# RWKV-7 / RG-LRU decoder step: two branch results kept in DRAM, weight halves asked for one tile ahead, sample steps spread over two units

## The chip, the cores and the metric

One NeuronCore of a Trainium2 chip runs the whole step as one program. The metric is device time in microseconds (us), lower is better. PE is TensorE's matmul stream, PEld its weight loads, DVE is VectorE, ACT is ScalarE, POOL is GpSimd, and SP is the queue of SyncE, which here issues every DMA. Instructions of one queue run in the order in which they stand in it; a waiting instruction holds all that stand behind it.

## The reference

One decoder layer in float32 for a prompt of 1024 tokens and 8 samples of one token each, which share all weights (D_MODEL 1024, D_FF 2816):

```python
def _layer(h, mk, mv, S0, shift0, h0, buf0, P):
    h = _layer_norm(DN_ALPHA * h + 0.5 * _swiglu(h, P['ffn1_wi'], P['ffn1_wo']), ...)
    mix, S_new, shift_new, h_new, buf_new = _mixer(h, S0, shift0, h0, buf0, P)
    h = _layer_norm(DN_ALPHA * h + mix, ...)
    h = _layer_norm(DN_ALPHA * h + _xattn(h, mk, mv, P['xa_wq'], P['xa_wo']), ...)
    h = _layer_norm(DN_ALPHA * h + 0.5 * _swiglu(h, P['ffn2_wi'], P['ffn2_wo']), ...)
```

The change is in the mixer, whose end is

```python
    yn = ((y - ym) * lax.rsqrt(yv + GN_EPS)).reshape(B, T, W) * gn_g + gn_b
    bonus = (jnp.sum(rh * kh * r_k, axis=-1, keepdims=True) * vh).reshape(B, T, W)
    rwkv_out = (yn + bonus) * g
    lru_out = hs * jax.nn.gelu(p_gelu)
    gates = jax.nn.sigmoid(p_gate).reshape(B, T, N_BRANCH, D_MODEL)
    merged = gates[:, :, 0] * rwkv_out + gates[:, :, 1] * lru_out
    out = merged @ P['w_mix_out']
```

Here `y` is the output of the RWKV-7 state recurrence and `hs` that of the RG-LRU branch. For a sample, one step of the recurrence is applied to its own 64 x 64 states: multiply by the decay, subtract and add outer products, read out.

## The kernel before

Activations lie transposed, channels on the 128 partitions and 1032 token columns (1024 prompt, 8 samples) along the free axis. A float32 product is made of three matmuls of two split halves (`mm3`, L125 to L127): hi x hi, hi x lo, lo x hi. A weight half of 128 x 512 is fetched by SP into a tile `raw` (L94), rounded by ACT into `wh` (L99), and DVE takes the rest, `wl` (L100); `split_half` does these three. A weight tile of 128 output channels is two such halves (`load_split`). `S.rawseq` and `S.hlseq` say which pools the next `raw` and the next `wh`, `wl` come from.

The program runs feed-forward 1, mixer, cross attention, feed-forward 2. In the mixer, channels are cut into 8 pairs of heads (p = 0 to 7), two of them at a time are a group g, and the prompt into 4 blocks n of 256 columns. A unit t = 4 g + n is one block of one group, so there are 16. One round per unit weaves these streams:

- `stage_unit` prepares unit t + 1 from the projections in the DRAM scratch `GD[p]` (tile `R`, `za`), and makes the bonus term `bv`;
- `inverse` solves the triangular systems of unit t, 31 dependent pairs of DVE instructions (`pr`, `tq`);
- `chain` runs the state recurrence of unit t - 1, and `post` normalises its output (`ysb`), adds `bv`, applies the gates `tg` and adds the branch's `lm`;
- `branches` makes the RG-LRU branch (`cb`, `ge`, `xc`, result `lm`) of unit t - 1;
- `samples_b` applies the samples' step, in rounds with n = 3, for both pairs of the group; for each pair and each half of the samples it needs five rows of DRAM scratch (`row`, L1142, tile `wt`, each as two DMAs) one after the other;
- `gemms` is the filler: the remaining input projections (`project`, tile `g`, stored by SP as `GD<-ev`, L639) and then the output projection (`out_proj`, `FD<-ev`).

`weave` and `rounds` set the order in which the code writes these; the framework's scheduler then sets each engine's queue, and every tile's pool says how many buffers it has and so which earlier reader a new writer waits for. Until the change, the filler had one `raw` buffer and three of `wh` and `wl`:

```python
        S.rawseq, S.hlseq = itertools.cycle([S.wraw]), itertools.cycle([S.whl])
```

The same two settings serve what comes after the rounds: `out_last` (last part of the output projection, with `f` and `acc` read from DRAM), its LayerNorm, and `memory_kv`, which makes keys and values of the 256 memory tokens (PSUM tile `kv`, weights `wk` and `wv`, results `mo` and `vo`), all woven into one another.

Of the kernel before, what the change touches and what calls it, by code (L numbers as in the profile page):

```python
# [10 lines left out]
F32 = mybir.dt.float32  # L11
F32R = mybir.dt.float32r
AF = mybir.ActivationFunctionType
ALU = mybir.AluOpType
# [5 lines left out]
NT = NP + NS  # L20
DFF = 2816
KT = D // 128
# [510 lines left out]
DRAM = bass.MemoryType.DRAM  # L533
GR, GK, GV, GZ, GA, GL, GE, G1, G0, GG = range(10)

FILL = [42] * 11 + [37] * 5

LATE = ("ev", "ref", "dend", "scl", "sm", "wsb", "sf", "ysb", "gsq", "ivc", "bv", "lm")


def mixer(octx, S, I, O, MG, HD, pre):
# [13 lines left out]
    with ExitStack() as ctx:  # L555
# [66 lines left out]
        FD = S.dram.tile([8, 128, NT], F32, name="FD")  # L622
        GD = [S.dram.tile([128, 10, NT], F32, name="GD%d" % p) for p in range(8)]

        def cols(w, c0, n, q, kt=KT):
            yield from settled(S, c0, n)
            for k in range(kt):
                mm3(nc, q, wblock(w, k), S.HH[:, k, c0:c0 + n], S.HL[:, k, c0:c0 + n], k == 0, k == kt - 1)
                if k % 2:
                    yield  # L630

        def project(p, mt, gi, func, sc, w, cs, psg, pool):

            for c0, n in cs:
                q = psg(n)
                yield from cols(w, c0, n, q)
                e = pool.tile([128, 344], F32, tag="ev", name="ev", bufs=2)[:, :n]
                ACT(e, q, func, scale=sc)
                nc.sync.dma_start(out=GD[p][:, gi, c0:c0 + n], in_=e)  # L639

# [15 lines left out]
        def gemms():  # L656


            for g in range(S.npairs // 2):
                ps_ = (2 * g, 2 * g + 1)  # L660
                for xs, early in (((0, 1, 2), True), ((3, 4, 5), False), ((6,), False)):
                    if g or not early:
                        for p in ps_:
                            for x in (tiles(p)[i] for i in xs):
                                yield from project(p, *x, load_split(S, I["w_in"][x[0]]), CH3, psg, t1)
                                ready.add((p, x[1]))
                            if 6 not in xs:
                                ends(p, early)
            ready.add("h")
            yield from out_proj()  # L670

# [108 lines left out]
        def stage(U, i):  # L780
# [52 lines left out]
            P.bv.append(bv)  # L833
            yield
# [122 lines left out]
        def branch(p, n, P):  # L957
# [38 lines left out]
            STT(gi, gi, 0.5, th, ALU.mult, ALU.mult)  # L996
            S.lm_live += 1
            assert S.lm_live <= 4
            hs = tmp("lm", 264, 4)
            nc.vector.tensor_tensor_scan(out=hs[:, 0:256], data0=gr[:, 0:256], data1=gi[:, 0:256],  # L1000
# [13 lines left out]
            STT(hs, ge[:, 1], 1.0, hs, ALU.add, ALU.mult)  # L1014
            P.lm.append(hs)
            if n == 3:
# [7 lines left out]
        def post(p, n, Y):  # L1024

            col = lambda t: t[:, p:p + 1]
            c0, P = NCW[n][0], Ps[p]
            while (p, G0) not in ready:
                yield
            tg = t1.tile([128, 2, 256], F32, tag="tg", name="tg")  # L1030
            nc.sync.dma_start(out=tg, in_=GD[p][:, G0:GG + 1, c0:c0 + 256])
# [10 lines left out]
            STT(ysb, ysb, col(V["gnb"]), P.bv[n][:, 0:256], ALU.add, ALU.add)  # L1042
            STT(tg[:, 0], tg[:, 0], 1.0, tg[:, 1], ALU.add, ALU.mult)
            yield
            while len(P.lm) <= n:
                yield
            STT(ysb, ysb, 0.5, tg[:, 0], ALU.mult, ALU.mult)
            STT(ysb, P.lm[n][:, 0:256], 0.5, ysb, ALU.mult, ALU.add)
            S.lm_live -= 1
# [79 lines left out]
        def samples_b(p, P):  # L1129

            y, T3 = tmp("y8", 8, 4, t1), P.T3
            P.y8 = y
            sv = P.sv
            b8 = lambda t: t.unsqueeze(2).to_broadcast([128, 4, 64])
            for b0 in (0, 4):
                B = slice(b0, b0 + 4)
                s_, t_ = (ta.tile([128, 4, 64], F32, tag=x, name=x) for x in ("ws", "wt"))
                nc.sync.dma_start(out=s_, in_=I["srwkv"][p].rearrange("p (b k) -> p b k", k=64)[:, B])

                def row(j):  # L1140
                    for h in range(2):
                        nc.sync.dma_start(out=t_[half[h]], in_=T3[8 * j + b0:8 * j + b0 + 4, 64 * h:64 * h + 64].unsqueeze(  # L1142
                            0).to_broadcast([64, 4, 64]))
                    return t_
# [7 lines left out]
                row(1)  # L1152
                yield
                TTo(s_, s_, t_, ALU.mult)
                row(4)
                yield
                TTo(t_, t_, b8(yb), ALU.mult)
                TTo(s_, s_, t_, ALU.subtract)
                row(2)
                yield  # L1160
                TTo(t_, t_, b8(sv[:, 5, B]), ALU.mult)
                TTo(s_, s_, t_, ALU.add)
                nc.sync.dma_start(out=O["srwkv"][p].rearrange("p (b k) -> p b k", k=64)[:, B], in_=s_)
                row(0)
                yield
                TTo(t_, s_, t_, ALU.mult)
                nc.vector.tensor_reduce(out=yb, in_=t_, axis=mybir.AxisListType.X, op=ALU.add)

# [30 lines left out]

        def out_proj():  # L1200

            kt = KT - 2
            for m in range(KT):
                w_ = load_split(S, I["w_mix"][m])
                for c0, n in CH3:
# [9 lines left out]
                    q = psg(n)  # L1215
                    yield from cols(w_, c0, n, q, kt)
                    e = tmp("ev", 344, 2)[:, :n]
# [28 lines left out]
        def stage_unit(t):  # L1246
            g, n = divmod(t, 4)
            U = SimpleNamespace(p0=2 * g, n=n, TT=TTs[t % 2], AR=[], SC=[], BK=[])
            if n == 0:
                U.ref = tmp("ref", 34, 2).rearrange("p (i c) -> p i c", i=2)  # L1250
                U.dend = tmp("dend", 32, 2).rearrange("p (i c) -> p i c", i=2)
                nc.vector.memset(U.ref[:, :, 16:17], 0.0)
                Ps.extend(SimpleNamespace(bv=[], lm=[]) for _ in range(2))
            else:
                U.ref, U.dend = units[-1].ref, units[-1].dend
# [26 lines left out]
        nu = 2 * S.npairs  # L1282
        nbr = S.lm_live = 0
        late_steps = []
        fill = gemms()
        rounds(13, [(stage_unit(0), 34), (part(fill, 42), 42)], late_steps, True)
        for t in range(nu):
# [405 lines left out]
```

## Time and profile before

| | |
|---|---|
| median of 3 runs | 3322.96 us (3314.7 to 3323.16) |
| profiled execution | 3323.29 us, of which the span from first to last instruction is 3321.4 us |
| mean granted TensorE clock | 0.942 of full speed |
| feed-forward 1, 0 to 660 us | PE busy 649.56 of 660 us, clock 1.00 |
| mixer's units, 860 to 2020 us | PE busy 1070.29 of 1160 us, clock 0.92 |
| last unit, 2020 to 2100 us | PE busy 53.65 of 80 us, clock 0.68 |
| end of the mixer, 2100 to 2200 us | PE busy 77.69 of 100 us, clock 0.81 |
| memory values, 2200 to 2280 us | PE busy 58.27 of 80 us, clock 0.58 |
| feed-forward 2, from 2640 us | PE busy 660.97 of 681 us, clock 0.98 |

Times in the profile count from the first instruction. "Busy" is the time in which an engine has an instruction in execution, and an instruction at half clock is busy for longer. "Idle before" is the time an engine stood still ahead of an instruction, with what ended it behind an arrow. The granted clock in a window is the mean over it.

### The profile page before, as it was taken

To read this page: it belongs to the slowest core of one execution; us is meant where nothing else is said; L and a number is where in the kernel's file an instruction comes from. 1 tells how busy PE (TensorE), PEld (TensorE's weight loads), DVE (VectorE), ACT (ScalarE), POOL (GpSimd) and SP (SyncE) were. 2 spreads that over 40 slices of the span, in tenths; PEclk is the share of its full clock that TensorE was granted. 3 is DMA by queue.
4 is the path that set the end of the run, shared out by engine and by line. 5 is a ranking of instruction groups with operands and counts; after the bars stand their busy time and mean duration, and the time that the engine had idled before them with its cause. 6 is when DMAs were issued, how large, how long until landed. Compare 5 with 4: busy or idle time off the path is not lost. (4 is left out here: it accounts for less than half of the span.)

```text
span 3321.4 us, 63119 instructions
## 1 busy us (share of the span) xinstructions
PE 3080.6 (93%) x23324; PEld 2896.4 (87%) x23324; DVE 2199.0 (66%) x5895; ACT 1433.5 (43%) x3190; POOL 554.5 (17%) x526
## 2 busy tenths in 40 slices
PE   8999999999999989989998987778898999999997
PEld 8999999989988878878887776667788899999997
DVE  7666665573377776778876777533768666666556
ACT  5333351145555555556554654343334433334112
POOL 2222201130000101100110100440003422220111
PEclk9999999999999999999998888768999999999998
DMA  4222253225433444444344444523533222225321
GB/s 136 77 78 80 84 166 112 87 80 175 152 108 105 123 128 120 112 117 139 104 123 121 115 115 136 161 84 118 153 121 120 79 77 77 80 80 163 112 83 52
DMA packets 364036, 369.93 MB, mean 111 GB/s; under 512 B 143024, under 2 KB 264912, under 8 KB 363728
## 3 DMA queue, kind: packets, MB, share of 16 engines
q1 hardware_dynamic: 363728, 365.91, 37.0%
q8 instruction: 183, 3.00, 0.4%
q14 instruction: 125, 1.02, 0.1%
HBM read 269.15 MB, written 96.84 MB: 110 GB/s over the span
## 5 line engine op out<-in xcount | busy, mean ns | idle before, releaser
L125 PE MATMUL ps<-HH,wh 128*128 128x258 f32 (+1 forms) x2384 | 718.4, 302 | 16.6 <-ACT HH L508 7.4
L126 PE MATMUL ps<-HL,wh 128*128 128x258 f32 (+1 forms) x2384 | 716.8, 301 | 0.6 <-POOL HL L215 0.6
L127 PE MATMUL ps<-HH,wl 128*128 128x258 f32 (+1 forms) x2384 | 715.6, 300 | 0.0
L125 PE MATMUL g<-HH,wh 128*128 128x344 f32 (+2 forms) x1840 | 628.9, 342 | 19.7 <-ACT wh L99 5.4
L126 PE MATMUL g<-HL,wh 128*128 128x344 f32 (+2 forms) x1840 | 602.2, 328 | 1.3 <-DVE HL L548 1.3
L127 PE MATMUL g<-HH,wl 128*128 128x344 f32 (+2 forms) x1840 | 598.8, 327 | 4.8 <-DVE wl L100 4.8
L125 PEld LDWEIGHTS ps<-HH,wh 128*128 128x128 f32 x2384 | 451.4, 189 | 18.7 <-ACT HH L508 7.4
L126 PEld LDWEIGHTS ps<-HL,wh 128*128 128x128 f32 x2384 | 451.0, 189 | 1.4 <-POOL HL L215 0.9
L127 PEld LDWEIGHTS ps<-HH,wl 128*128 128x128 f32 x2384 | 450.5, 189 | 0.0
L125 PEld LDWEIGHTS g<-HH,wh 128*128 128x128 f32 x1840 | 361.7, 197 | 39.8 <-ACT wh L99 9.7
L127 PEld LDWEIGHTS g<-HH,wl 128*128 128x128 f32 x1840 | 360.4, 196 | 12.2 <-DVE wl L100 7.9
L126 PEld LDWEIGHTS g<-HL,wh 128*128 128x128 f32 x1840 | 361.9, 197 | 7.6 <-DVE HL L548 3.5
L228 ACT ACTIVATE wh<-raw 128x512 fp32r<-128x512 f32 x280 | 176.5, 631 | 322.2 <-PE ps L126 259.5
L100 DVE TENSOR_TENSOR wl<-raw,wh 128x512 fp32r<-128x512 f32 x302 | 214.0, 714 | 152.9 <-ACT wh L99 150.7
L99 ACT ACTIVATE wh<-raw 128x512 fp32r<-128x512 f32 x302 | 185.9, 626 | 294.8 <-PE ps L126 77.2
L334 POOL TENSOR_TENSOR raw<-raw 128x512 f32<-128x512 f32 x160 | 213.8, 1336 | 566.1 <-DVE wl L229 372.6
L229 DVE TENSOR_TENSOR wl<-raw,wh 128x512 fp32r<-128x512 f32 x280 | 203.8, 729 | 139.6 <-ACT wh L228 132.7
L442 DVE SCALAR_TENSOR_TENSOR acc<-ps,acc 128x344 f32<-128x344 f32 x336 | 168.5, 512 | 144.2 <-PE ps L127 143.6
L548 DVE TENSOR_TENSOR pr<-tq,iv 128x2 f32<-128x2 f32 (+30 forms) x496 | 160.8, 324 | 3.0
L553 ACT ACTIVATE ev<-g 128x344 f32<-128x344 f32 x192 | 87.3, 455 | 133.0 <-PE g L127 108.1
L917 DVE TENSOR_REDUCE tq<-pr 128x1 f32<-128x2 f32 (+30 forms) x496 | 121.6, 245 | 2.9
L374 ACT ACTIVATE g<-g 128x258 f32<-128x258 f32 x160 | 67.1, 419 | 112.9 <-DVE g L333 112.0
(410 smaller groups left out, 6444.9 us busy)
## 6 DMA issues: line engine op xcount, KB each, us to landing
raw<-in_wi_dram SPq DMA_DIRECT2D x176, 256.0 KB, 2.8
raw<-in_w_in_dram SPq DMA_DIRECT2D x116, 256.0 KB, 3.4
GD<-ev SPq DMA_DIRECT2D x168, 172.0 KB, 1.9
raw<-in_wo_dram SPq DMA_DIRECT2D x104, 256.0 KB, 3.1
raw<-HID SPq DMA_DIRECT2D x88, 258.0 KB, 3.1
HID<-g SPq DMA_DIRECT2D x80, 258.0 KB, 2.1
wt<-T SPq DMA_DIRECT2D x160, 64.0 KB, 2.7
GD<-t SPq DMA_DIRECT2D x24, 344.0 KB, 3.5
```

The costliest lines, as they stand in the source:

```text
L99: nc.scalar.activation(out=hi, in_=raw, func=AF.Identity)
L100: nc.vector.tensor_tensor(out=lo, in0=raw, in1=hi.bitcast(F32), op=ALU.subtract)
L125: nc.tensor.matmul(ps, wh, xh, start=first, stop=False)
L126: nc.tensor.matmul(ps, wh, xl, start=False, stop=False)
L127: nc.tensor.matmul(ps, wl, xh, start=False, stop=last)
L228: nc.scalar.activation(out=hi, in_=x, func=AF.Identity)
L229: nc.vector.tensor_tensor(out=lo, in0=x, in1=hi.bitcast(F32), op=ALU.subtract)
L334: pool_tt = lambda o, a, b, op: nc.gpsimd.tensor_tensor(out=o, in0=a, in1=b, op=op)
L442: nc.vector.scalar_tensor_tensor(out=a, in0=q, scalar=0.5 / ALPHA, in1=a, op0=ALU.mult, op1=ALU.add)
L548: TTo = lambda o, a, b, op: nc.vector.tensor_tensor(out=o, in0=a, in1=b, op=op)
L553: ACT = lambda o, a, f=AF.Identity, **kw: nc.scalar.activation(out=o, in_=a, func=f, **kw)
L917: nc.vector.tensor_reduce(out=tq[:, 0:m, i], in_=pv, axis=mybir.AxisListType.X, op=ALU.add)
```

## The change

It does five things, all in the mixer.

- `bv` (32 stores of 128 x 256) and `lm` (32 stores) go to two new planes of `GD[p]`, GB and GM; `post` reads them back with the gates, in one DMA of four planes in place of two, and begins only when the branch's block is there. Their tiles shrink from 8 to 2 and from 4 to 2 buffers.
- A fourth buffer of `wh` and `wl` is put into the filler's cycle, and `project` and `out_proj` ask for one half of the next weight tile after the matmuls of the first and of the second of their three column chunks, instead of both halves ahead of the tile.
- `row` has two buffers, and rows are fetched two at a time, ahead of their use.
- `samples_b` runs for one pair in the round with n = 3 and for the other in the round after it; in the last round still for both.
- After the rounds, two more `raw` buffers and one more of `wh` and `wl` (`more_weights`).

```diff
-GR, GK, GV, GZ, GA, GL, GE, G1, G0, GG = range(10)
+GR, GK, GV, GZ, GA, GL, GE, G1, G0, GG, GB, GM = range(12)
...
-        def project(p, mt, gi, func, sc, w, cs, psg, pool):
+        def project(p, mt, gi, func, sc, w, cs, psg, pool, then=None):
             for c0, n in cs:
                 q = psg(n)
                 yield from cols(w, c0, n, q)
+                if then and c0 < CH3[2][0]:
+                    then()
                 e = pool.tile([128, 344], F32, tag="ev", name="ev", bufs=2)[:, :n]
...
+            queue = itertools.chain(((W[j], x[:, 512 * i:512 * i + 512]) for j, x in enumerate(src) for i in range(2)))
+            def load():
+                for to, x in itertools.islice(queue, 1):
+                    to.append(split_half(S, x))
+            load()
+            load()
+            for j, (p, x, i) in enumerate(todo):
+                yield from project(p, *x, W[j], CH3, psg, t1, load)
...
-        S.rawseq, S.hlseq = itertools.cycle([S.wraw]), itertools.cycle([S.whl])
+        S.rawseq = itertools.cycle([S.wraw])
+        S.hlseq = itertools.cycle([S.whl] * 3 + [actx.enter_context(tc.tile_pool(name="mwhl", bufs=1))])
...
-            bv = tmp("bv", 256, 8)
+            bv = tmp("bv", 256, 2)
             TTo(bv, xv[:, 0:256], pb[:, 0:256], ALU.mult)
+            nc.sync.dma_start(out=GD[p][:, GB, c0:c0 + 256], in_=bv)
...
-            hs = tmp("lm", 264, 4)
+            hs = tmp("lm", 264, 2)
...
-            P.lm.append(hs)
+            nc.sync.dma_start(out=GD[p][:, GM, c0:c0 + 256], in_=hs[:, 0:256])
+            P.lm.append(n)
...
-            while (p, G0) not in ready:
+            while (p, G0) not in ready or n not in P.lm:
                 yield
-            tg = t1.tile([128, 2, 256], F32, tag="tg", name="tg")
-            nc.sync.dma_start(out=tg, in_=GD[p][:, G0:GG + 1, c0:c0 + 256])
+            tg = t1.tile([128, 4, 256], F32, tag="tg", name="tg")
+            nc.sync.dma_start(out=tg, in_=GD[p][:, G0:GM + 1, c0:c0 + 256])
...
                 def row(j):
+                    t = ta.tile([128, 4, 64], F32, tag="wt", name="wt", bufs=2)
                     for h in range(2):
...
-                row(3)
-                yield
-                TTo(t_, s_, t_, ALU.mult)
-                nc.vector.tensor_reduce(out=yb, in_=t_, axis=mybir.AxisListType.X, op=ALU.add)
+                r3 = row(3)
+                r1 = row(1)
+                yield
+                yield
+                TTo(r3, s_, r3, ALU.mult)
+                nc.vector.tensor_reduce(out=yb, in_=r3, axis=mybir.AxisListType.X, op=ALU.add)
+                r4 = row(4)
...
-            if n == 3:
-                s.append((pairs_of(samples_b, g), 21))
-            elif n == 1 and g:
+            if t == nu - 1:
+                s.append((pairs_of(samples_b, g), 25))
+            elif n == 3 or (n == 0 and t):
+                p = (t - 1) // 2 if n == 0 else 2 * g
+                s.append((samples_b(p, Ps[p]), 13))
+            if n == 1 and g:
                 s.append((pairs_of(samples_c, g - 1), 10))
...
         S.norms = Norms(S, octx)
+        more_weights(S, ctx, 2, 1)
```

How the queues stand, at three places. First, SP in the middle of round 3 (the first with samples); before:

```order
L1142 DMA wt<-T_13075 64x4x64 x2
L639 DMA GD_8806<-ev 128x344
L94 DMA raw<-in_w_in_dram 128x512
L1163 DMA out_srwkv_dram<-ws 128x256
L1142 DMA wt<-T_13075 64x4x64 x2
L639 DMA GD_8806<-ev 128x344
L94 DMA raw<-in_w_in_dram 128x512
L875 DMA D_13221<-SC_13529 32x4x32 x2
```

The same place after:

```order
L94 DMA raw<-in_w_in_dram 128x512
L641 DMA GD_8806<-ev 128x344
L1152 DMA wt<-T_13095 64x4x64 x4
L94 DMA raw<-in_w_in_dram 128x512
L641 DMA GD_8806<-ev 128x344
L1060 DMA MG<-ysb 128x256
L844 DMA GD_8806<-bv 128x256
L1043 DMA tg<-GD_8805 128x4x256
```

The rows come four DMAs (two rows) at a time instead of two, with other transfers between, and a store of `bv` now stands in the queue.

Second, SP in the last round, about the last `cb` load of the branch; before:

```order
L1138 DMA ws<-in_srwkv_dram 128x256
L1142 DMA wt<-T_24151 64x4x64 x2
L1008 DMA out_lru_dram<-hl 128x9
L972 DMA cb<-GD_8811 128x267
L974 DMA ge<-GD_8811 128x2x264
L1219 DMA FD<-ev 128x344
```

After:

```order
L1152 DMA wt<-T_24267 64x4x64 x3
L94 DMA raw<-in_w_mix_dram 128x512
L1231 DMA FD<-ev 128x344
L1019 DMA out_lru_dram<-hl 128x9
L1026 DMA GD_8810<-lm 128x256
L985 DMA cb<-GD_8811 128x267
L987 DMA ge<-GD_8811 128x2x264
```

Ahead of `cb` there still stand rows, and besides them a store of `lm`.

Third, ACT where `memory_kv` makes the values; before:

```order
L207 ACTIVATE acc<-acc,lnb 128x264
L214 ACTIVATE HH<-acc 128x264
L99 ACTIVATE wh<-raw 128x512
L1371 ACTIVATE vo<-kv 128x256 x2
L99 ACTIVATE wh<-raw 128x512 x4
```

After:

```order
L1388 ACTIVATE vo<-kv 128x256 x2
L183 ACTIVATE lnq<-acc 128x256 x2
L99 ACTIVATE wh<-raw 128x512
L183 ACTIVATE lnq<-acc 128x256
L99 ACTIVATE wh<-raw 128x512 x3
L1388 ACTIVATE vo<-kv 128x256 x2
L99 ACTIVATE wh<-raw 128x512
L195 ACTIVATE lnx<-lnv 128x256
```

The value weights stood alone behind the LayerNorm of the third block (`acc`, `HH`); now they stand among that LayerNorm's squares (`lnq`).

More of the change, by code (lines that the diff above doesn't have):

```diff
@@ L533 @@
 DRAM = bass.MemoryType.DRAM
-GR, GK, GV, GZ, GA, GL, GE, G1, G0, GG = range(10)
+GR, GK, GV, GZ, GA, GL, GE, G1, G0, GG, GB, GM = range(12)
 FILL = [42] * 11 + [37] * 5
-LATE = ("ev", "ref", "dend", "scl", "sm", "wsb", "sf", "ysb", "gsq", "ivc", "bv", "lm")
+LATE = ("ev", "ref", "dend", "scl", "sm", "wsb", "sf", "ysb", "gsq", "ivc", "lm")
 def mixer(octx, S, I, O, MG, HD, pre):
@@ L622, in mixer @@
         FD = S.dram.tile([8, 128, NT], F32, name="FD")
-        GD = [S.dram.tile([128, 10, NT], F32, name="GD%d" % p) for p in range(8)]
+        GD = [S.dram.tile([128, 12, NT], F32, name="GD%d" % p) for p in range(8)]
         def cols(w, c0, n, q, kt=KT):
@@ L656, in gemms @@
         def gemms():
+            todo = []
             for g in range(S.npairs // 2):
[L660 to L668, printed above, removed]
+                for xs in ((0, 1, 2), (3, 4, 5), (6,)):
+                    if g or xs[0]:
+                        todo += [(p, tiles(p)[i], i) for p in (2 * g, 2 * g + 1) for i in xs]
+            src = [I["w_in"][x[0]] for _, x, _ in todo] + [I["w_mix"][m] for m in range(KT)]
+            W = [[] for _ in src]
+            queue = itertools.chain(((W[j], x[:, 512 * i:512 * i + 512]) for j, x in enumerate(src) for i in range(2)))
[6 more added lines that the diff above has]
+                yield from project(p, *x, W[j], CH3, psg, t1, load)
+                ready.add((p, x[1]))
+                if i in (2, 5):
+                    ends(p, i == 2)
             ready.add("h")
-            yield from out_proj()
+            yield from out_proj(W[len(todo):], load)
         with ExitStack() as c2:
@@ L996, in branch @@
             STT(gi, gi, 0.5, th, ALU.mult, ALU.mult)
-            S.lm_live += 1
-            assert S.lm_live <= 4
-            hs = tmp("lm", 264, 4)
+            hs = tmp("lm", 264, 2)
             nc.vector.tensor_tensor_scan(out=hs[:, 0:256], data0=gr[:, 0:256], data1=gi[:, 0:256],
@@ L1041, in post @@
             yield
-            STT(ysb, ysb, col(V["gnb"]), P.bv[n][:, 0:256], ALU.add, ALU.add)
+            STT(ysb, ysb, col(V["gnb"]), tg[:, 2], ALU.add, ALU.add)
             STT(tg[:, 0], tg[:, 0], 1.0, tg[:, 1], ALU.add, ALU.mult)
             yield
-            while len(P.lm) <= n:
-                yield
             STT(ysb, ysb, 0.5, tg[:, 0], ALU.mult, ALU.mult)
-            STT(ysb, P.lm[n][:, 0:256], 0.5, ysb, ALU.mult, ALU.add)
-            S.lm_live -= 1
+            STT(ysb, tg[:, 3], 0.5, ysb, ALU.mult, ALU.add)
             if p < S.npairs - 2:
@@ L1136, in samples_b @@
                 B = slice(b0, b0 + 4)
-                s_, t_ = (ta.tile([128, 4, 64], F32, tag=x, name=x) for x in ("ws", "wt"))
+                s_ = ta.tile([128, 4, 64], F32, tag="ws", name="ws")
                 nc.sync.dma_start(out=s_, in_=I["srwkv"][p].rearrange("p (b k) -> p b k", k=64)[:, B])
                 def row(j):
+                    t = ta.tile([128, 4, 64], F32, tag="wt", name="wt", bufs=2)
                     for h in range(2):
-                        nc.sync.dma_start(out=t_[half[h]], in_=T3[8 * j + b0:8 * j + b0 + 4, 64 * h:64 * h + 64].unsqueeze(
+                        nc.sync.dma_start(out=t[half[h]], in_=T3[8 * j + b0:8 * j + b0 + 4, 64 * h:64 * h + 64].unsqueeze(
@@ L1143, in row @@
                             0).to_broadcast([64, 4, 64]))
-                    return t_
+                    return t
                 yb = y[:, B]
-                row(3)
+                r3 = row(3)
+                r1 = row(1)
                 yield
-                TTo(t_, s_, t_, ALU.mult)
-                nc.vector.tensor_reduce(out=yb, in_=t_, axis=mybir.AxisListType.X, op=ALU.add)
+                yield
+                TTo(r3, s_, r3, ALU.mult)
+                nc.vector.tensor_reduce(out=yb, in_=r3, axis=mybir.AxisListType.X, op=ALU.add)
@@ L1151, in samples_b @@
+                r4 = row(4)
                 TSC(yb, yb, 0.5, None, ALU.mult, None)
-                row(1)
+                TTo(s_, s_, r1, ALU.mult)
+                r2 = row(2)
                 yield
-                TTo(s_, s_, t_, ALU.mult)
-                row(4)
                 yield
-                TTo(t_, t_, b8(yb), ALU.mult)
-                TTo(s_, s_, t_, ALU.subtract)
-                row(2)
+                TTo(r4, r4, b8(yb), ALU.mult)
+                TTo(s_, s_, r4, ALU.subtract)
@@ L1160, in samples_b @@
+                r0 = row(0)
+                TTo(r2, r2, b8(sv[:, 5, B]), ALU.mult)
+                TTo(s_, s_, r2, ALU.add)
+                nc.sync.dma_start(out=O["srwkv"][p].rearrange("p (b k) -> p b k", k=64)[:, B], in_=s_)
                 yield
[L1161 to L1164, printed above, removed]
                 yield
-                TTo(t_, s_, t_, ALU.mult)
@@ L1167, in samples_b @@
-                nc.vector.tensor_reduce(out=yb, in_=t_, axis=mybir.AxisListType.X, op=ALU.add)
+                TTo(r0, s_, r0, ALU.mult)
+                nc.vector.tensor_reduce(out=yb, in_=r0, axis=mybir.AxisListType.X, op=ALU.add)
         def samples_c(p, P):
@@ L1198, in samples_c, with out_proj @@
                 direct(p, NP, NS, y)
-        def out_proj():
+        def out_proj(W, load):
             kt = KT - 2
             for m in range(KT):
-                w_ = load_split(S, I["w_mix"][m])
                 for c0, n in CH3:
@@ L1215, in out_proj @@
                     q = psg(n)
-                    yield from cols(w_, c0, n, q, kt)
+                    yield from cols(W[m], c0, n, q, kt)
+                    if c0 < CH3[2][0]:
+                        load()
                     e = tmp("ev", 344, 2)[:, :n]
@@ L1252, in stage_unit @@
                 nc.vector.memset(U.ref[:, :, 16:17], 0.0)
-                Ps.extend(SimpleNamespace(bv=[], lm=[]) for _ in range(2))
+                Ps.extend(SimpleNamespace(lm=[]) for _ in range(2))
             else:
@@ L1282, in mixer @@
         nu = 2 * S.npairs
-        nbr = S.lm_live = 0
+        nbr = 0
         late_steps = []
```

1 line of the change is left out of this document (removed).

## The prediction

> **What bounds the kernel now.** I read the busy shares in equal slices first: PE is nearly full in both feed-forwards and is not in the mixer. So I cut the mixer into windows: three double rounds without samples' steps (the first, third and fifth row), three with them (second, fourth, sixth), rounds 13 and 14 with the start of 15, the last round, the end of the mixer, the memory values, and the first queries.
>
> ```profile
> span 3321.4 us, 63119 instructions
> ```
>
> ```profile
> core 0: us, PE busy (x) PEld busy (x) DVE busy (x) ACT busy (x) POOL busy (x), PEclk, DMA share, GB/s
> 969.20:1099.00 129.80, 122.95 (x1114) 110.63 (x1112) 97.38 (x339) 74.88 (x177) 13.18 (x14) 0.99 0.38 106
> 1099.00:1261.70 162.70, 146.71 (x1163) 129.70 (x1164) 118.47 (x393) 87.80 (x193) 11.21 (x13) 0.90 0.45 125
> 1261.70:1395.40 133.70, 126.19 (x1145) 113.41 (x1143) 101.70 (x368) 77.64 (x186) 18.32 (x17) 0.98 0.42 116
> 1395.40:1553.00 157.60, 142.27 (x1138) 126.67 (x1138) 116.94 (x388) 92.19 (x194) 11.01 (x12) 0.90 0.46 126
> 1553.00:1684.40 131.40, 125.89 (x1121) 113.42 (x1121) 101.84 (x362) 76.34 (x182) 15.66 (x15) 0.97 0.41 112
> 1684.40:1848.30 163.90, 148.73 (x1159) 128.17 (x1156) 121.48 (x402) 84.07 (x191) 12.93 (x14) 0.88 0.44 120
> 1848.30:2020.00 171.70, 153.86 (x1197) 126.43 (x1195) 134.74 (x476) 96.88 (x225) 18.22 (x16) 0.85 0.44 121
> 2020.00:2100.00 80.00, 53.65 (x414) 43.99 (x414) 47.41 (x140) 30.14 (x66) 4.68 (x4) 0.68 0.44 118
> 2100.00:2202.40 102.40, 78.34 (x468) 70.96 (x467) 62.56 (x147) 44.63 (x113) 65.68 (x82) 0.82 0.47 145
> 2202.40:2266.50 64.10, 47.76 (x181) 39.32 (x180) 13.58 (x23) 16.53 (x36) 6.02 (x8) 0.52 0.27 83
> 2266.50:2284.00 17.50, 13.85 (x87) 12.94 (x86) 5.61 (x10) 5.79 (x12) 0.00 (x0) 0.80 0.37 118
> ```
>
> Two losses add up here: PE stands still, and it runs at a low granted clock. The rounds with samples' steps have about as many matmuls as the others (1138 to 1163 against 1114 to 1145) and take (162.7 + 157.6 + 163.9) / 3 = 161.4 us against (129.8 + 133.7 + 131.4) / 3 = 131.6 us: 29.8 us more each, at clock 0.88 to 0.90 instead of 0.97 to 0.99. The memory values run at 0.52.
>
> Now who waits, first in the memory values (the waits of PE from 2100 us to the queries, then those of ACT in the values' window), with the sizes of the steps:
>
> ```profile
> PE kv L125 <- ACT wh L99: 20.0, 20, 2.2
> ...
> ACT wh L99 <- DMA raw<-in_wv_dram: 30.9, 9, 4.9
> ...
> raw<-in_wv_dram SPq DMA_DIRECT2D x16, 256.0 KB, 2.5
> ...
> L100 DVE TENSOR_TENSOR wl<-raw,wh 128x512 fp32r<-128x512 f32 x302 | 214.0, 714 | 152.9 <-ACT wh L99 150.7
> L99 ACT ACTIVATE wh<-raw 128x512 fp32r<-128x512 f32 x302 | 185.9, 626 | 294.8 <-PE ps L126 77.2
> ...
> L125 PE MATMUL kv<-wh,memh x60: 281/415/583, 2202.4 to 2266.2; 128*128 128x256 f32 x60
> L1371 ACT ACTIVATE vo<-kv x8: 378/381/383, 2214.5 to 2267.1; 128x256 f32<-128x256 f32 x8
> ...
> 2226.22 0.41 PE L125 MATMUL kv<-wh,memh 128*128 128x256 f32 x1
> 2226.43 0.41 PE L126 MATMUL kv<-wl,memh 128*128 128x256 f32 x1
> ...
> 2284.30 0.28 PE L125 MATMUL g<-HH,wh 128*128 128x256 f32 x1
> 2284.42 0.28 PE L126 MATMUL g<-HL,wh 128*128 128x256 f32 x1
> ```
>
> A value half takes four of each kind of matmul, so 60 are 15 halves in 64.1 us, 4.27 us each. One `raw` buffer explains that: transfer 2.5, `wh` 0.63, `wl` 0.71, sum 3.84, and the rest is handing over. PE needs 12 matmuls per half: 0.21 us apart at half clock (2226.22 to 2226.43) is 2.55 us, 0.12 apart at full clock (2284.30 to 2284.42) is 1.44 us. The feed sets the pace and PE waits in every half.
>
> Then the last round, in order of time on five queues:
>
> ```profile
> 2040.31 1.24 SPq L1142 DMA_DIRECT2D wt<-T  x2
> 2042.29 0.38 SPq L972 DMA_DIRECT2D cb<-GD  x1
> 2043.76 0.43 DVE L548 TENSOR_TENSOR wt<-ws,wt 128x256 f32<-128x256 f32 x1 [3.48 <-DMA wt<-T]
> 2044.49 0.61 ACT L553 ACTIVATE xc<-cb,vec 128x264 f32<-128x264 f32 x1 [7.32 <-DMA cb<-GD]
> 2044.67 1.25 SPq L1142 DMA_DIRECT2D wt<-T  x2
> 2046.96 1.22 PE L985 MATMUL m<-xc,wg 128*128 128x264 f32 x2 [9.05 <-DVE xc L549]
> 2049.73 1.36 SPq L1142 DMA_DIRECT2D wt<-T  x2
> ```
>
> With one row buffer, the next row can be asked for only when DVE has read the last one, and SP stands at that wait. `cb` is behind it on SP, ACT waits 7.32 us for `cb`, and PE 9.05 us for what follows. Rows come 4.36 and 5.06 us apart.
>
> **The change part by part.** The sum goes against the profiled execution, 3323.29 us (span 3321.4), which is 0.3 us above the median of the three runs.
>
> *T1, values: more raw buffers.* Three slots instead of one make the feed 4.27 / 3 = 1.42 us a half. Each of the four value groups empties its only bank `kv` with two ACT passes of 0.38 us, about 1.2 us with the start again, 5 in all. If PE gets its full clock: 15 x 1.44 + 5 = 27 us, a gain of 37. If it stays at half clock: 15 x 2.55 + 5 = 43, a gain of 21. I take 30, since the feed now shares DMA and ACT with the LayerNorm, among which the values stand in the new order.
>
> The row says that the clock is 0.52 though PE's longest wait there is 2.2 us. The Trainium skill (TensorE: Matmul & The Clock Gate, "What's actually happening") says that the gate goes down after an idle window of about 3.4 us and comes back after a busy one of that length. By that rule a steady feed warms PE and T1 is 37; by the row alone, which shows no recovery, it is 21. The rest of the sum is the same for both, 3233 or 3249.
>
> *T2, the stretch before, 2100 to 2202 us.* At full clock PE's work is 78.34 x 0.82 = 64 of 102.4 us. 20.0 us of waits for `wh` on `kv` lie in both windows; the values' 15 halves at 0.9 are 13.4 of them, so 6.6 are here. I take 12, that wait and as much for the clock; ends 0 and 38 (all idle and cold time gone). What is late next is POOL, busy 65.68 us here.
>
> *T3, first queries.* 13.85 x 0.80 = 11 of 17.5 us: ends 0 and 6; 2.
>
> *T4, last round.* PE's work at full clock is 53.65 x 0.68 = 36 of 80 us. The code has 2 pairs x 2 halves x 5 rows = 20 row steps one after another; rows in pairs leave 3 latencies per half, 12 in all. At 4.36 to 5.06 us (mean 4.7) the eight that go are 38 us of chain. The recurrence and the inverse run beside it and are not shortened, so I take 18; ends 0 and 38.
>
> *T5, the other three rounds with samples.* Against their neighbours they lose 3 x 29.8 = 89 us. About 17 us of that is DVE work in each (118.47 against 101.70), which stays and only moves by a round; the rest are the same waits as in T4. I take 8 each, 24; ends: 60, and a loss of 9 if the rounds with n = 0 have no room on DVE.
>
> *T6, the fourth half and the asking ahead.* The waits of PE on filler weights from 860 to 2100 us, and that of ACT:
>
> ```profile
> PE g L127 <- DVE wl L100: 4.5, 5, 2.3
> ...
> PE g L125 <- ACT wh L99: 2.4, 4, 1.4
> ...
> ACT wh L99 <- DMA raw<-in_w_in_dram: 42.9, 28, 6.3
> ```
>
> PE loses 6.9 us. ACT waits much more, but the single `raw` stays, so ACT can still come to `wh` before its transfer lands: 4, ends 0 and 12.
>
> *T7, cost of the way by DRAM.* 64 more stores on SP, and `tg` with four planes instead of two. Their nearest kin:
>
> ```profile
> L639 SPq DMA_DIRECT2D GD<-ev x168: 319/338/1472, 747.7 to 1874.8; - x168
> L1031 SPq DMA_DIRECT2D tg<-GD x32: 370/427/1293, 971.7 to 2094.4; - x32
> ...
> SPq L639 <- ACT ev L553: 168.8, 78, 7.2
> ```
>
> Issue is 64 x 0.34 = 22 us on SP, spread over 16 rounds and hidden while SP's queue has room. The real cost is the wait: a store waits for DVE to finish `bv` or `lm`, and everything behind it on SP waits too, the next `raw`, `R`, `za`, `cb`. The kin waits 168.8 / 78 = 2.2 us each time. `post` needs its `tg` two steps later than it asks for it, so that DMA is covered; if it weren't, it would cost the chain's end in the last two units. Cost 7, ends 0 and 64 x 2.2 = 141. I take a low value because SP already stands at such waits for every `ev` and PE has little to do with them.
>
> Sum: -30 - 12 - 2 - 18 - 24 - 4 + 7 = -83, 3323.3 - 83 = 3240 us.
>
> **The rivals.**
> - *The rounds keep their length* (0.20). Another wait on DVE takes the place of the rows: DVE is busy 118 of 163 us there, in bursts, and `inverse` is 31 dependent pairs whatever the samples do. For it: the samples' DVE work is all still there. Against: the 9.05 us of PE hang on an SP wait, not on DVE work. Then T4 and T5 are nothing, T1, T2, T3, T6 and T7 remain: -41, 3282 us.
> - *Clock and waits go together* (0.13). Where gaps close, the low clock goes with them, as in the double rounds at 0.97 to 0.99. T1 37, T2 25, T3 4, T4 28, T5 40, T6 6, T7 5: -135, 3188 us.
> - *The change does nothing that counts* (0.04). The mixer's end is set by POOL's and DVE's LayerNorm, and the values merely move under it while that gets longer. For it: POOL's 65.68 us. Against: POOL has 6.02 in the values' window. 3318 us.
> - *SP becomes the bound* (0.05), the case that ends slower. The place is the stage of each unit, where `bv`'s store stands ahead of the next loads. At the full 2.2 us per store: 3323 - 90 + 141 = 3374 us. It decides from 90 / 64 = 1.4 us per store that reach PE.
>
> **How the numbers follow.** My forecast has 0.58, the rivals 0.20, 0.13, 0.04 and 0.05. The prediction is 3240 us. The range 3188 to 3296 holds the forecast and the rounds that keep their length with their spread, and the near half of the case with the clock; it leaves out about 0.17. Change of less than 0.3% (10 us) can't be told from none here. Faster 0.91 (0.58 + 0.20 + 0.13), same 0.04, slower 0.05.
>
> **What would show it.** T1, T2: waits of PE `kv` for `wh` under 5 us in all, clock over 0.8 in the values; the first queries, at 2266 us now, begin some 80 us earlier. T4: no wait of PE near 9 us in the last round, and rows two by two on SP. T5: double rounds with samples under 155 us, those without still about 131. T6: PE's waits for filler `wl`, `wh` under 3 us. T7: SP's waits at the stores of `bv` and `lm` short, and waits for `R`, `za` and `cb` on ACT and DVE no longer than now. I'd be wrong if the clock stays near 0.5 with the feed mended, if DVE is as long in the way, or if SP's new stores show as long waits ahead of loads.

## The result, and the profile after

| | median | against before |
|---|---|---|
| before | 3320.34 us (3314.7 to 3323.16, 4 runs) | |
| changed | 3219.4 us (3217.57 to 3223.72, 4 runs) | 0.970, 95% interval 0.9682 to 0.9718 |

The change makes the kernel 101 us shorter; 83 were forecast. The profiled execution of the changed kernel took 3223.72 us.

```profile
span 3221.9 us, 63123 instructions
```

The windows of the changed kernel, cut as before was. The first, third and fifth rows are double rounds without a first half of the samples, the second, fourth and sixth those with it (the second half now runs in their second round); then come rounds 13 and 14, the last round, the keys, the values and the first queries.

```profile
core 0: us, PE busy (x) PEld busy (x) DVE busy (x) ACT busy (x) POOL busy (x), PEclk, DMA share, GB/s
969.70:1100.50 130.80, 125.05 (x1131) 113.00 (x1130) 97.94 (x341) 75.73 (x178) 12.81 (x13) 0.99 0.45 124
1100.50:1251.60 151.10, 141.68 (x1206) 125.23 (x1207) 118.17 (x391) 88.42 (x193) 13.51 (x14) 0.97 0.53 147
1251.60:1389.40 137.80, 129.59 (x1125) 114.80 (x1124) 101.59 (x370) 78.68 (x188) 17.38 (x16) 0.98 0.45 128
1389.40:1540.80 151.40, 139.05 (x1150) 122.77 (x1149) 116.31 (x385) 83.96 (x185) 11.94 (x12) 0.94 0.52 144
1540.80:1676.20 135.40, 130.31 (x1143) 116.03 (x1142) 103.17 (x375) 79.49 (x189) 18.47 (x16) 0.99 0.47 132
1676.20:1827.70 151.50, 140.56 (x1162) 119.99 (x1161) 114.94 (x386) 81.64 (x181) 10.78 (x12) 0.93 0.53 141
1827.70:1972.30 144.60, 124.94 (x903) 102.17 (x902) 109.37 (x381) 86.39 (x205) 17.57 (x15) 0.81 0.45 129
1972.30:2065.30 93.00, 71.50 (x529) 61.10 (x528) 68.41 (x230) 38.64 (x81) 10.39 (x9) 0.78 0.57 155
2065.30:2133.90 68.60, 58.26 (x475) 52.95 (x474) 51.44 (x119) 35.21 (x89) 41.87 (x54) 0.96 0.68 205
2133.90:2163.70 29.80, 28.91 (x229) 28.50 (x229) 22.98 (x41) 16.60 (x38) 13.58 (x16) 0.92 0.72 219
2163.70:2181.00 17.30, 15.82 (x116) 15.19 (x115) 10.44 (x22) 10.19 (x26) 7.61 (x10) 0.90 0.35 112
```

The double rounds with samples are some 10 us shorter (151 instead of 161 us), those without 1 to 4 longer, and rounds 13 and 14 take 144.6 us instead of 136.7. The large gain stands in the last four rows. The values' window has PE busy 28.91 of 29.80 us at clock 0.92; before it was 47.76 of 64.1 at 0.52.

The matmuls of keys (`memh,wh`) and values (`wh,memh`), first of before, then of the changed kernel (duration min/median/max in ns, first and last start):

```profile
L125 PE MATMUL kv<-memh,wh x64: 276/280/580, 2105.1 to 2190.6; 128*128 128x256 f32 x64
L125 PE MATMUL kv<-wh,memh x64: 281/415/583, 2194.7 to 2266.2; 128*128 128x256 f32 x64
```

```profile
L125 PE MATMUL kv<-memh,wh x64: 278/280/467, 2065.3 to 2126.1; 128*128 128x256 f32 x64
L125 PE MATMUL kv<-wh,memh x64: 276/281/415, 2134.1 to 2163.5; 128*128 128x256 f32 x64
```

From these rows and the starts of the rounds (1985.0 and 1972.3 for round 15) comes where the time went:

| stretch | before | after | difference |
|---|---|---|---|
| rounds 1 to 14 | 1015.8 us | 1002.6 | -13.2 |
| round 15 to the first key matmul | 120.1 | 93.0 | -27.1 |
| keys | 85.5 | 60.8 | -24.7 |
| between keys and values | 4.1 | 8.0 | +3.9 |
| values | 71.5 | 29.4 | -42.1 |
| all behind them | | | +3 |

PE's waits for weights in the changed kernel, 860 to 2100 us, and behind that for `kv`, 2100 to 2184:

```profile
PE g L125 <- ACT wh L99: 19.0, 7, 6.7
PE g L127 <- DVE wl L100: 6.5, 3, 3.3
...
PE kv L125 <- ACT wh L99: 2.2, 1, 2.2
```

`kv` waits 2.2 us instead of 20.0, as forecast. The filler `g` waits 25.5 us instead of 6.9, where I had forecast under 3. The longest of these waits, on SP and then on PE:

```profile
2020.51 1.24 SPq L1152 DMA_DIRECT2D wt<-T  x2
2021.85 0.55 SPq L1174 DMA_DIRECT2D out_srwkv_dram<-ws  x1
2022.49 0.38 SPq L94 DMA_DIRECT2D raw<-in_w_mix_dram  x1
```

```profile
2026.64 0.66 PE L125 MATMUL g<-HH,wh 128*128 128x344 f32 x1 [6.66 <-ACT wh L99]
```

`raw` stands on SP behind the samples' rows and their result, and PE waits 6.66 us for what follows from it. From this I concluded at first that the asking ahead was worth nothing. The experiments say otherwise.

### The profile page after: what moved, and what is told of

Same layout as the page of the kernel before. It is cut to its first block, busy times and chain, and to the rows that moved or that the text cites. A ratio compares the mean times of both kernels' runs of the same rounds, so it can differ in the third digit from the quotient of the medians.

```text
span 3221.9 us, 63123 instructions
## 1 busy us (share of the span) xinstructions
PE 3029.4 (94%) x23324; PEld 2855.4 (89%) x23324; DVE 2199.8 (68%) x5895; ACT 1433.5 (44%) x3192; POOL 560.8 (17%) x526
## 5 line engine op out<-in xcount | busy, mean ns | idle before, releaser
L125 PE MATMUL g<-HH,wh 128*128 128x344 f32 (+2 forms) x1840 | 625.0, 340 | 31.5 <-ACT wh L99 20.3
```

Source lines behind the costliest of these rows:

```text
L125: nc.tensor.matmul(ps, wh, xh, start=first, stop=False)
```

## The experiments

Four parts can be put on and taken off: the way by DRAM (T7), the fourth half with the asking ahead (T6), the samples' rows in pairs and their spread over two rounds (T4, T5), and the buffers at the end (T1 to T3). The tiles that the way by DRAM frees make the room for the new buffers, so the other parts were tried on top of it; the spread, which needs no buffer, was not tried without it. Times are medians, ratios go against the executions of before that were measured beside each run, and a ratio step of 0.01 is 33 us. "Rounds" is rounds 1 to 14, "end" is round 15's start to the last value matmul, both of the one profiled execution; as the four executions of the way by DRAM alone spread over 26 us, differences of a few us in these two columns say little.

| run | time, us | ratio, 95% interval | rounds | end |
|---|---|---|---|---|
| before | 3320.34 | | 1015.8 | 281.8 |
| changed | 3219.4 | 0.970 (0.9682 to 0.9718) | 1002.6 | 191.7 |
| way by DRAM alone | 3381.55 | 1.0179 (1.0136 to 1.0222) | 1060.7 | 290.5 |
| stores alone | 3369.14 | 1.0126 (1.0105 to 1.0147) | 1054.0 | 289.6 |
| way by DRAM, stores on POOL | 3370.85 | 1.0149 (1.0126 to 1.0172) | 1045.5 | 289.8 |
| way by DRAM, more buffers | 3390.13 | 1.0196 (1.0174 to 1.0217) | 1066.1 | 293.2 |
| way by DRAM, fourth half | 3368.9 | 1.0130 (1.0106 to 1.0154) | 1056.6 | 284.8 |
| the same, asking ahead | 3322.44 | 1.0009 (0.9996 to 1.0023) | 1007.6 | 288.2 |
| way by DRAM, buffers at the end | 3307.35 | 0.9977 (0.9960 to 0.9993) | 1068.6 | 225.0 |
| changed, no buffers at the end | 3294.12 | 0.9927 (0.9908 to 0.9947) | 998.5 | 270.4 |
| changed, samples unspread | 3270.18 | 0.9845 (0.9824 to 0.9866) | 1042.8 | 191.8 |
| changed, single rows | 3278.87 | 0.9878 (0.9851 to 0.9904) | 1008.9 | 233.0 |
| changed, raw by POOL | 3213.49 | 0.9657 (0.9631 to 0.9683) | 990.4 | 195.7 |
| changed, rows by POOL | 3190.84 | 0.9582 (0.9555 to 0.9609) | 974.6 | 188.5 |

### The way by DRAM alone

```diff
 # before, and:
-            bv = tmp("bv", 256, 8)
+            bv = tmp("bv", 256, 2)
...
+            nc.sync.dma_start(out=GD[p][:, GB, c0:c0 + 256], in_=bv)
...
-            hs = tmp("lm", 264, 4)
+            hs = tmp("lm", 264, 2)
...
+            nc.sync.dma_start(out=GD[p][:, GM, c0:c0 + 256], in_=hs[:, 0:256])
...
-            while (p, G0) not in ready:
+            while (p, G0) not in ready or n not in P.lm:
...
-            tg = t1.tile([128, 2, 256], F32, tag="tg", name="tg")
+            tg = t1.tile([128, 4, 256], F32, tag="tg", name="tg")
```

> Before with the way by DRAM alone: bv and lm stored to the two new planes, tg read with four, no other part. Theory A (the gain is made in the last round and behind it, by the raw buffers and by SP being free of single rows; the way by DRAM costs next to nothing, as SP's 30 waits of 0.5 to 2.4 us at the new stores in the changed kernel's trace are mostly in SP's idle time): 3315 to 3330 us, within 0.3% of before, kv still waits about 20 us for wh and the values still take over 60 us. Rival B (the way by DRAM itself brings something, because post no longer holds bv and lm and eight buffers of bv let the stages run apart): 3290 to 3310. Rival C (T7 was under-sized and other parts pay for it): 3340 or more, with longer waits for R, za or cb.

It takes 65 us more by the medians than the 3316.88 of before beside it, 59 by the ratio. Theory A falls; the third case, T7 under-sized, is what happened, though without the longer waits for loads that it named (below). The rounds, before and with the way by DRAM:

```profile
969.20:1985.00 1015.80, 934.99 (x7814) 820.71 (x7812) 762.00 (x2614) 571.27 (x1309) 99.17 (x97) 0.92 0.43 118
```

```profile
971.50:2032.20 1060.70, 960.40 (x7810) 842.15 (x7808) 770.21 (x2617) 562.49 (x1304) 98.98 (x97) 0.90 0.45 128
```

The matmuls are the same to four; they are busy for 25 us longer at a lower clock, and PE stands 20 us more. Three runs ask why.

```diff
 # 1: stores alone: before with the two stores; post keeps bv and lm in 8 and 4 buffers
 # 2: way by DRAM, stores issued by POOL
-            nc.sync.dma_start(out=GD[p][:, GB, c0:c0 + 256], in_=bv)
+            nc.gpsimd.dma_start(out=GD[p][:, GB, c0:c0 + 256], in_=bv)
   (and the store of lm likewise)
 # 3: way by DRAM, more buffers
-            bv = tmp("bv", 256, 2)
+            bv = tmp("bv", 256, 6)
...
-            hs = tmp("lm", 264, 2)
+            hs = tmp("lm", 264, 4)
```

> Before with the 64 stores of bv and lm on SP and nothing else: post still takes both from its 8 and 4 buffers, tg stays at two planes. The way by DRAM in full took 65 us (3381.55 against 3316.88), and POOL's queue for the stores took back some 10 of them only. Theory P (SP's waits at the stores cost, wherever they stand): 3365 to 3390. Theory Q (the cost is on the reading side: post begins only when lm is there, waits for four planes, and with it the order of PE's and DVE's work is laid out anew): 3315 to 3335.

> The way by DRAM alone as in the run that took 3381.55 us, with the 64 stores of bv and lm issued by POOL's queue instead of SP's. Theory P (the 65 us that the way by DRAM costs are SP standing at its new stores with raw, R, za and cb behind them): most of the 65 us go, 3315 to 3340. Theory O (they come from where the instructions of PE and DVE now stand, since the reads of tg wait for lm and the scheduler lays the rounds out anew; PE's waits for filler weights grew by 2 us only): still 3355 to 3390. POOL is busy some 99 us of the rounds, so it has room for 64 issues.

> The way by DRAM alone, with bv in 6 buffers instead of 2 and lm in 4 instead of 2 (8 of bv have no room). If the cost comes from the shrunk tiles (a new bv or lm has to wait until the store before the last has left): 3315 to 3340 us. If it comes from the stores on SP or from the new order of the instructions: 3360 to 3390.

The stores alone carry 1.26 of the 1.79 per cent, so the reading side and the smaller tiles have at most the rest, and theory Q falls. More buffers bring nothing, so the shrunk tiles are not the reason. The stores on POOL's queue bring 10 us by the ratios, and the intervals overlap, so most of it is not that SP is held at them either, though the time of the stores alone lies where theory P had it. The waits say the same: SP's in the rounds sum to 603 us, against 586 before; ACT waits for `raw` 40.7 us, against 36.8, and all waits of ACT and DVE for `R`, `za` and `cb` sum to 8.3 us, against 6.0. Nor is it the added traffic by itself: with the asking ahead, in the next section, the DMA share in the rounds is higher still (0.48 against 0.45) and the rounds are 53 us shorter. What grows is waiting between the engines: the waits of PE for other engines that the profile lists sum to 97.7 us instead of 78.7, DVE's to 260.7 instead of 222.7. The filler also stands on PE in fewer bunches between the chains' matmuls: counted in the trace, 296 in the rounds instead of 308. So the rows speak for a new order on PE and DVE. That is argued by leaving the rest out, not shown: no run restored the old order, and which instruction's place it hangs on was not found.

### The fourth half and the asking ahead

```diff
 # way by DRAM, fourth half
-        S.rawseq, S.hlseq = itertools.cycle([S.wraw]), itertools.cycle([S.whl])
+        S.rawseq = itertools.cycle([S.wraw])
+        S.hlseq = itertools.cycle([S.whl] * 3 + [actx.enter_context(tc.tile_pool(name="mwhl", bufs=1))])
 # and then the asking ahead (here of project; out_proj likewise)
+                yield from project(p, *x, W[j], CH3, psg, t1, load)
```

> The way by DRAM with the fourth half of wh and wl, without the asking one tile ahead. The two together brought 59 us (3381.55 to 3322.44). Theory A (the fourth half does it, since both halves of a tile can be made while the tile before is still in use): 3320 to 3340. Theory B (the asking ahead does it, since with the old asking both halves are asked for in one go and the single raw and the place in SP's queue stay as they are): 3365 to 3385.

> The way by DRAM with the fourth half of wh and wl and the asking one tile ahead; rows one by one and samples as before, no buffers more at the end. Theory A (asking ahead is worth nothing while the single raw is issued by SP in order, behind stores and rows that wait for DVE): within 6 us of the run with the way by DRAM alone, PE's waits of g for wh and wl stay near or over the 6.9 us of before instead of falling under 3. Rival B (T6 as predicted; the new waits of 20 us that the changed kernel shows come from the rows four at a time, not from the asking ahead): 4 to 12 us below the run with the way by DRAM alone, those waits under 3 us.

The buffer alone brings 16 us by the ratios (the intervals overlap a little), the asking ahead 40 more, so theory B of the first run holds; the asking ahead with three halves was not tried. Together they give back nearly all that the way by DRAM costs, 59 us by the medians. In the second run both sizes fall, theory A's by a factor of ten, and the waits do not go under 3 us as rival B had it. The rounds of this run:

```profile
970.10:1977.70 1007.60, 932.98 (x7809) 812.46 (x7807) 763.54 (x2622) 567.12 (x1315) 99.56 (x97) 0.95 0.48 135
```

What misled me were the waits for weights. First the run with the way by DRAM alone, then this one, 860 to 2280 us:

```profile
PE g L125 <- ACT wh L99: 4.6, 4, 3.6
PE g L127 <- DVE wl L100: 1.1, 4, 0.4
ACT wh L99 <- DMA raw<-in_w_in_dram: 45.8, 30, 5.4
```

```profile
PE g L125 <- ACT wh L99: 11.9, 6, 5.1
PE g L127 <- DVE wl L100: 2.6, 5, 0.8
ACT wh L99 <- DMA raw<-in_w_in_dram: 39.3, 30, 2.7
```

The run that is 53 us shorter in its rounds waits longer for weights on PE. The gain is not in that row. With weights asked for early the scheduler can put the filler in smaller pieces between the chains, 352 bunches instead of 296: two groups of PE show it, one of the state recurrence and one of `stage_unit`, by the loss ahead of `y<-SC,QZ` (2.7 us in before) and of `m<-ident,s` (20.1 in before), way by DRAM first:

```profile
L1086 PE MATMUL y<-SC,QZ 128*64 128x64 f32 x458 | 36.6, 240 | 11.1 <-DVE QZ L1080 10.1 <-DVE iv L909 0.8
L775 PE MATMUL m<-ident,s 128*128 128x128 f32 x56 | 14.0, 332 | 23.3 <-ACT s L553 23.3
```

```profile
L1099 PE MATMUL y<-SC,QZ 128*64 128x64 f32 x456 | 33.1, 234 | 4.6 <-DVE QZ L1093 4.2 <-DVE iv L922 0.4
L788 PE MATMUL m<-ident,s 128*128 128x128 f32 x56 | 13.5, 326 | 18.6 <-ACT s L553 14.4 <-DVE wl L100 2.5 <-DVE xc L549 1.7
```

11 us of PE's 26 us of regained standing are in these two groups; another 27 us are the clock, 0.95 instead of 0.90. That the finer bunches cause this fits, but was only read, not tried by itself, and their number alone does not decide: with the samples unspread, in the next section, there are 344 and the rounds take 1042.8 us.

### Rows in pairs, and the spread

```diff
 # samples unspread: changed, with both pairs in the round n = 3 as before (weight in weave 25; before 21)
+            if n == 3:
+                s.append((pairs_of(samples_b, g), 25))
+            elif n == 1 and g:
...
 # single rows: changed, with row() in one buffer as before (weights 21 and 11 instead of 25 and 13)
-                    t = ta.tile([128, 4, 64], F32, tag="wt", name="wt", bufs=2)
+                s_, t_ = (ta.tile([128, 4, 64], F32, tag=x, name=x) for x in ("ws", "wt"))
```

> The changed kernel with both pairs' samples in the round n = 3, rows still two at a time. Theory A (of the 28 us between the run without buffers at the end, 3294, and the run with the way by DRAM and the asking ahead, 3322, the larger part is the rows two at a time, and about 15 to 20 of it lies in the last round): less than 10 us longer than the changed kernel, 3217 to 3230. Theory B (the spread over two rounds brings the larger part, since DVE's work of the samples is halved in a round): 12 to 25 us longer, 3232 to 3245, with rounds 3, 7 and 11 back near 84 us.

> The changed kernel with rows one at a time, samples still spread over two rounds. Theory A (the rows carry the gain, above all in the last round, where 20 latencies of 4.4 to 5.1 us stand one after the other again): 15 to 30 us longer than the changed kernel, 3235 to 3250, from round 15 to the end of kv some 15 us longer. Theory B (the spread carries it): less than 10 us longer, 3217 to 3230.

Both lose more than either theory gave, 48 and 59 us by the ratios, and at different places. Unspread, the end is the changed kernel's (191.8 us), and the rounds are 40 us longer. With single rows, the rounds are 6 us longer, and the end 41 us. The rows of the last round, issued by SP, first with single rows, then the changed kernel:

```profile
L1151 SPq DMA_DIRECT2D wt<-T x40: 573/580/1070, 1971.9 to 2099.1; - x40
```

```profile
L1152 SPq DMA_DIRECT2D wt<-T x36: 573/594/926, 1976.6 to 2038.0; - x36
```

The last of them goes out at 2038.0 instead of 2099.1, 61 us earlier, and 56 if both are counted from the start of round 15. (Four of the changed kernel's 40 lie ahead of the window.) So T4 is the rows in pairs. What stands last in that round shows it too, PE's waits from the start of round 15 to the keys with single rows:

```profile
PE m L1188 <- DVE y L1176: 8.8, 1, 8.8
...
PE m L998 <- DVE xc L549: 3.5, 2, 2.7
```

PE stands 8.8 us for the samples' result `y`, the end of the chain of rows; the changed kernel has no such wait. T5 is smaller than it looks: against the run with the asking ahead (1007.6 us, neither rows nor spread) the spread alone gives 1008.9, pairs alone 1042.8, and both 998.5 or 1002.6. Why pairs that are not spread lose 35 us in the rounds stays open (their weight in the weave differs, too, and was not tried by itself); the unspread rounds 3, 7 and 11 take 97 to 98 us there, against 84 to 86 with single rows.

### The buffers at the end

```diff
 # way by DRAM, buffers at the end (added); changed, no buffers at the end (taken away)
         S.norms = Norms(S, octx)
+        more_weights(S, ctx, 2, 1)
```

> The way by DRAM and the two raw buffers and one of wh and wl after the rounds, nothing else of the change (without the way by DRAM the buffers have no room). Theory A: the values take 30 to 35 us instead of 64 at a clock near 1, kv's wait for wh falls from 20 to under 3 us, some of the stretch before them goes too: 45 to 60 us below the run with the way by DRAM alone, so 3260 to 3275. Rival B (the raw buffers only move the wait: what the values gain, POOL and the LayerNorm of the mixer's end take, and the gain behind the rounds comes from the last round being shorter): 3295 to 3315.

> The changed kernel without the raw buffers and the half more after the rounds. Theory A (T1 and T2 are the largest part): 45 to 60 us longer than the changed kernel, 3265 to 3280 us, kv waits for wh about 20 us again, values over 60 us at a clock near 0.5. Rival B (the values were slow because they came after the LayerNorm, and the new rounds put them elsewhere): less than 20 us longer, 3220 to 3240, values at a clock over 0.8 with the single raw buffer.

They bring 74 us by the medians (67 by the ratios) beside the way by DRAM alone, and are 75 us of the changed kernel; the end shortens by 66 and 79 us. That is the largest part. Theory A had the mechanism both times and too small a size (45 to 60). The 3307.35 us lie where rival B of the first run had them only because both times were reckoned from a way by DRAM that costs nothing. In the run without them the values' matmuls have a median of 415 ns and take 68.0 us; with them on the way by DRAM alone:

```profile
L125 PE MATMUL kv<-memh,wh x64: 276/280/582, 2161.3 to 2233.3; 128*128 128x256 f32 x64
L125 PE MATMUL kv<-wh,memh x64: 276/281/388, 2235.9 to 2264.8; 128*128 128x256 f32 x64
```

The values take 28.9 us there, in the old order of the rest. So rival B of the second run, that their place in the order did it, is out, and rival B of the first, that the buffers only move the wait, as well.

### Two queues for what waits on SP

```diff
 # rows by POOL: changed, and in row()
-                        nc.sync.dma_start(out=t[half[h]], ...
+                        nc.gpsimd.dma_start(out=t[half[h]], ...
 # raw by POOL: changed, and for the rounds
+        S.wdma = nc.gpsimd
```

> The changed kernel with the rows issued by POOL's queue, so that raw no longer stands behind rows that wait for DVE on SP. Theory A (PE's 20 us of waits for filler wh in eight gaps of up to 6.7 us come from that queue): those waits fall under 8 us and the time by 8 to 20 us, 3200 to 3212. Rival B (raw then stands behind ev, the stores of bv and lm and out_srwkv, which wait for DVE and ACT just as long): within 6 us of the changed kernel. Rival C (POOL's own work of the round, ivs, ivc and v, is held by the rows that wait for DVE): 3230 or more, with PE's waits for s and gsq longer.

> The changed kernel with raw issued by POOL's queue in the rounds, rows and the rest on SP as they are. Theory A: raw stands behind no store and no row, PE's waits for filler wh and wl fall under 8 us in all from 26.8, and the time by 8 to 20 us, 3200 to 3212. Rival B (the single raw buffer, which DVE and ACT must have read, holds raw on whatever queue): within 6 us of the changed kernel. Rival C (POOL's queue is held by raw's wait for DVE's wl, and ivs and ivc come late): 3230 or more.

The rows on POOL's queue bring 39 us by the ratios, 29 by the medians, and make the fastest version here, 3190.84 us, more than theory A gave. PE's waits for filler `wh` with the rows on POOL, 860 to 2280 us, and the rows there:

```profile
PE g L125 <- ACT wh L99: 3.9, 3, 2.1
```

```profile
L1152 POOL DMA_DIRECT2D wt<-T x129: 615/615/783, 1092.1 to 1945.6; - x129
```

The changed kernel has 20.3 us in that window. They become 3.9, and the rounds 28 us shorter, in 363 bunches of filler instead of 337. In the changed kernel's rounds SP's 35 waits at the rows sum to 48.1 us. The Trainium skill (Trainium Kernel Development and Optimization, "Key Constraints") says that issuing from several engines only saves the sequencer's issue time. These runs show more than that: here the second queue takes the waits, too, out of the way of what stands behind them. It need not be all queue: the scheduler lays the rest out anew as well, and the two were not separated. With `raw` on POOL the same waits, with those for `wl`, fall from 26.8 to 2.8 us, yet the run is only 14 us shorter by the ratios (6 by the medians), and the two intervals just touch. So theory A has the waits right there, the time does not decide between it and rival B, and the weights' wait itself is the smaller part of what the rows on SP cost.

## Why the prediction was right, and where it was not

The sum came out near because its larger terms, at the end, had mostly the right causes and were too small by 28 us together, and because in the rounds two errors of more than 50 us cancelled, which left those terms too large by 8. The first is a sound mechanism with a cautious size; the second is luck.

- *T1, values: mechanism right, size too small.* Forecast 30 with ends 21 and 37; the values went from 71.5 to 29.4 us, 42. The window began at 2202.4 us and the values at 2194.7, so one half of sixteen and its stretch were left out of the count. For the fifteen halves that were counted, the time went from 64.1 to 25.6 us, 38, at clock 1.00: the end of 37, with PE at its full clock, was right, and the 30 in the middle was not. PE got its clock back (0.52 to 0.92 in the windows) once the feed was steady. That is what the Trainium skill's rule (TensorE: Matmul & The Clock Gate, "What's actually happening") would make of it. Why waits of at most 2.2 us had held the clock at half stays open.
- *T2, the stretch before: too small.* Forecast 12 of at most 38. The keys alone gave 24.7. They pass by the same `raw`: with the buffers at the end alone they fall from 86.9 to 72.0 us. The rest goes with the rows in pairs, since the changed kernel with single rows takes 73.3 us for the keys. I had counted the 6.6 us that PE waits there and as much for the clock, instead of the keys' feed as I did for the values'.
- *T3, first queries: nothing.* 17.5 to 17.3 us, forecast 2. They begin 102 us earlier (2164 instead of 2266); 80 was forecast.
- *T4, last round: too small.* Forecast 18 of at most 38; 27.1 us from round 15 to the keys. Taking the rows' pairs away costs 34.5 there, from 93.0 to 127.5, close to the 38 of chain. The recurrence beside it did not hold it up. The 9.05 us wait of PE became 2.3, but the rows in pairs are not what took it away: with single rows it is 2.7, and the long wait, 8.8 us, stands at the samples' result instead. Nor did SP stand at a row ahead of that `cb`, as I had read it; its waits of 1.4 and 1.5 us there are at the samples' states, the store and the next load of `ws`.
- *T5, three double rounds: wrong cause.* Forecast 24. The three did become 10 us shorter each, but the run with the asking ahead has nearly the same (156.6, 152.3 and 151.1 us) without rows in pairs or spread. Rows and spread together brought 5 to 9 us in all rounds.
- *T6: wrong by more than ten times.* Forecast 4 of at most 12, priced by PE's waits for weights. On top of the way by DRAM it is 59 us, while those waits grow. The step that failed is the bound: a wait for a tile shows what the order now loses, not what another order could gain.
- *T7: wrong by eight to nine times, inside its ends.* Forecast 7 of 0 to 141; alone it is 59 to 65 us, 1.0 us per store, not far from the 1.4 where the rival with SP decided. I called it hidden because SP's waits hurt little. SP is indeed for the most part not the way it costs, by the run with the stores on POOL. In the changed kernel's rounds SP does wait 57 us at the new stores, up to 4.3 us (not 2.4, as I read it before the first run), yet the waits for `R`, `za` and `cb` sum to 5.6 us, against 6.0. What the sum had no term for is a new order on PE and DVE, for which the rows above speak.
- T6 and T7 together: forecast +3, measured +6. They cancel, which is why the total hid both; nothing in the working foresaw that.

The rival that the rounds keep their length was nearly right for the rounds (13 us of 1016), and its 3282 us failed on the end. Clock and waits going together came true at the end, not in rounds 13 and 14, which are at 0.81 (0.85 before) and 8 us longer.

## What to carry to other kernels

Where a scheduler sets the order, price a part by a run with it alone: waits for a tile are no bound on what a new place of the request does to everything woven around it, and two parts of a change can hide 60 us in each other. Where PE waits a little in every weight half, look at the whole stretch that shares the buffer (with the buffers at the end alone, values 44 us shorter and keys 15), and price it at the full clock as well. Try to move what waits for a slow engine out of the queue that feeds PE: moving the samples' rows off SP gave another 29 to 39 us here, part of which may be the new order.

## What the runs showed of the hardware that was not expected

- PE's clock returned in full with a feed that has no regular gap: the values' matmuls went from a median of 415 to 281 ns, and their window from 0.52 to 0.92 (1.00 from the second half on), though DMA rose from 83 to 219 GB/s in it.
- A DMA issued by POOL counts in the profile as that engine's work: 129 rows of 615 ns, against 594 to 614 ns on SP's queue. POOL's busy time in the rounds rose from 102.46 to 181.58 us, and ACT's waits for POOL's `ivs` only from 39.4 to 46.2 us.
